# Hybrid decoder block on one core: two of four weight sums by accumulating DMAs, memory keys turned by TensorE

## The chip, the cores and the metric

The kernel runs on one core of a Trainium2 chip. Its time is the device time of one execution in microseconds (us). Engines are named TensorE (PE in the rows; PEld is its weight load), VectorE (DVE), ScalarE (ACT), GpSimd (POOL) and SyncE (SP, which here only issues DMAs; SPq is its queue). Each engine works through its own list of instructions in order and waits at semaphores for the others.

## The reference, cut to what matters

All is float32, with 256 tokens (S), 256 memory tokens and a model width of 2048.

```python
h = rmsnorm(x, g_mix[l])
z = h @ w_in[l]                       # 2048 x 12288: q|k|v, u|v, memory q, three gates
...
kvm = rmsnorm(mem, g_mem[l]) @ w_mem_kv[l]
km, vm = jnp.split(kvm, 2, axis=-1)
km = rmsnorm(km.reshape(B, M, N_HEADS_M, HEAD_DIM_M), gk_m[l])     # 4 heads of 256
...
merged = (ga * (ya @ w_branch[l, 0]) + gb * (yb @ w_branch[l, 1])
          + gm * (ym @ w_branch[l, 2]))
x = x + merged @ w_out[l]
hf = rmsnorm(x, g_ffn[l])
gt, up = jnp.split(hf @ w_gate_up[l], 2, axis=-1)                  # two halves of 5632 columns
x = x + (jax.nn.silu(gt) * up) @ w_down[l]
```

## The kernel before, in words

**Products.** A weight matrix comes in units of 512 KB (128 partitions x 2 blocks of 128 rows x 512 columns), one DMA each, issued by SP into one of six buffers `raw`. Each operand is split in two parts of type fp32r: ScalarE copies `raw` to `whi` (line 128), VectorE makes `wlo = raw - whi` (line 129), and each product is three matmuls, hi x hi, hi x lo, lo x hi. There are four `whi` and four `wlo` buffers. `product` (line 142) runs one column block of 512 for both halves of the tokens, 12 matmuls for a unit.

**The hidden stage.** `hidden(j)`, j from 0 to 10, makes 512 columns of the gate and the same 512 of the up projection with `fast_pair`. It walks over eight pairs of units, `src0[kp]` and `src1[kp]`. An ordinary pair costs 24 matmuls. For some pairs (`sums`) the 2x2 blocks of tokens and of weights are multiplied by a scheme of seven products in place of eight (21 matmuls), which needs four sums of weight blocks: `ta[0] = raw1[0] - raw0[0]`, `ta[1] = raw1[1] - raw1[0]`, `tb[0] = raw1[1] - ta[0]`, `tb[1] = raw0[1] - tb[0]`. `ta` and `tb` are then split like weights, into tiles `both`. The products are banks P1 to P7: P1 and P2 use raw0, P3 raw1, P5 and P7 use ta, P6 and P4 use tb. TensorE takes them in the order P1, P2, P3, P5, P7, P6, P4. Such sum blocks are the pairs 0, 2 and 4 for j from 2, pair 4 for j = 0, and pairs 0 and 4 for j = 1: 30 in all. After the last, `u2` to `u4` combine P1 to P7 on VectorE. `ta` lies in the pool's only buffer with tag "v"; the tile `v`, in which an activation is put together after its transposing DMA (`turn_end`, line 263), uses the same buffer. `tb` takes one of the six `raw` buffers.

**Around it.** `back` multiplies finished activations with w_down, between the hidden stages; its results are added into `xr` (line 634). Work handed to `defer` is emitted some units later.

**Turning.** To exchange rows and columns of a 128-row tile, `turn_start` splits it into two planes of 16-bit halves (VectorE, line 259) and SP issues transposing DMAs (line 261); `turn_end` joins the halves on ScalarE (line 265). `heads` does so with the normalised queries and keys, and VectorE then scales them by the gain (line 362).

**What sets the order.** The program is written in the order in which the functions are called; the tile framework's scheduler then sets each engine's list of instructions from it, by its own estimates of when what is ready, and places the semaphores. The instructions of a pair may therefore stand in another order than in the code.

Of the kernel before, what the change touches and what calls it, by code (L numbers as in the profile page):

```python
# [9 lines left out]
F32 = mybir.dt.float32  # L10
F32R = mybir.dt.float32r
U16 = mybir.dt.uint16
AF = mybir.ActivationFunctionType
ALU = mybir.AluOpType
AX = mybir.AxisListType

P = 128
S = 256
NT = S // P
# [10 lines left out]
NK = 2  # L30
# [8 lines left out]
def hybrid_block(ctx: ExitStack, tc: tile.TileContext, x, xT, memr, memT_in, gains, g_sgu, w_sguT, w_in, w_mem_kv,  # L39
                 w_branch, w_out, w_gate_up, w_down, out):  # L40
    nc = tc.nc

    cp = ctx.enter_context(tc.tile_pool(name="cp", bufs=1))
# [10 lines left out]
    def bigt(shape, dtype=F32, nm="big"):  # L54
        return big.tile(shape, dtype, tag="big", name=nm)
# [10 lines left out]
    def acct():  # L66
        return ps_acc.tile([P, NC], F32, tag="acc", name="acc")

    def smt():
        return ps_sm.tile([P, NC], F32, tag="sm", name="sm")  # L70
# [4 lines left out]

    gT = cp.tile([P, NGAIN], F32, name="gT")
    nc.scalar.dma_start(gT, gains)
    mhalf = cp.tile([P, 16], F32, name="mhalf")
    nc.vector.memset(mhalf, -0.5)
    warm = cp.tile([P, 16], F32, name="warm")  # L80
# [2 lines left out]
    for nm, n, s in (("qa", 1, 128.0 ** -0.5), ("qm", 2, 256.0 ** -0.5), ("b", 8, 0.5)):  # L83
# [9 lines left out]
                            pattern=[[-1, P]], channel_multiplier=1)  # L93
    nc.gpsimd.affine_select(out=dist[:, P:3 * P], in_=dist[:, P:3 * P], compare_op=ALU.is_ge, fill=1e33, base=P,
                            pattern=[[-1, 2 * P]], channel_multiplier=1)

    def gcol(nm, i=0):
        return gT[:, GAINS[nm] + i:GAINS[nm] + i + 1]
# [7 lines left out]
    def defer(f, units=1):  # L106

        later.append((clock[0] + units, f))
# [18 lines left out]
    def split_w(raw, hi, lo):  # L127
        nc.scalar.activation(hi, raw, AF.Copy)  # L128
        nc.vector.tensor_tensor(out=lo, in0=raw, in1=hi.bitcast(F32), op=ALU.subtract)  # L129
# [7 lines left out]
    def load_w(src):  # L137

        raw, hi, lo = unit_tiles()
        nc.sync.dma_start(raw, src.rearrange("p (k n) -> p k n", k=NK))  # L140
        split_w(raw, hi, lo)
        return hi, lo
# [28 lines left out]
    def fast_pair(src0, src1, quads, sums):  # L171

        P1, P2, P3, P5, P7, P6, P4, X = range(8)
        banks = {i: (ps_x.tile([P, NC], F32, tag="x", name="x") if i < 2 else acct()) for i in range(8)}  # L180
        npair = 2 * len(quads)
        uses = {b: [] for b in banks}
        for kp in range(npair):
            for b in (range(7) if kp in sums else (P2, P2, P3, P3, P4, P4, X, X)):
                uses[b].append(kp)
        done = {b: 0 for b in banks}

        def mm(b, a, w):

            first, done[b] = done[b] == 0, done[b] + 1  # L190
            last = done[b] == len(uses[b])
            nc.tensor.matmul(banks[b], a[0], w[0], start=first, stop=False)  # L192
            nc.tensor.matmul(banks[b], a[0], w[1], start=False, stop=False)  # L193
            nc.tensor.matmul(banks[b], a[1], w[0], start=False, stop=last)  # L194

        def split_t(t):
            both = bigt([P, 2, NK, NC], F32R, "both")
            split_w(t, both[:, 0], both[:, 1])
            return both[:, 0], both[:, 1]

        for kp in range(npair):
            q, c = quads[kp // 2], 2 * (kp % 2)

            def blk(i, t):
                return q[:, 0, c + i, t * P:(t + 1) * P], q[:, 1, c + i, t * P:(t + 1) * P]

            if kp not in sums:
                for src, b0, b1 in ((src0, P2, P4), (src1, P3, X)):
                    hi, lo = load_w(src[kp])
                    tick()  # L210
                    for i in range(NK):
                        w = hi[:, i, :], lo[:, i, :]
                        mm(b0, blk(i, 0), w)
                        mm(b1, blk(i, 1), w)
                continue
            sm = sums[kp]
            sk = [(sm[:, 0, i, :], sm[:, 1, i, :]) for i in range(4)]
            raw0, hi0, lo0 = unit_tiles()
            raw1, hi1, lo1 = unit_tiles()
            nc.sync.dma_start(raw0, src0[kp].rearrange("p (k n) -> p k n", k=NK))  # L220
            nc.sync.dma_start(raw1, src1[kp].rearrange("p (k n) -> p k n", k=NK))
            split_w(raw0, hi0, lo0)
            split_w(raw1[:, 1, :], hi1[:, 1, :], lo1[:, 1, :])
            ta = tr.tile([P, NK, NC], F32, tag="v", name="ta", bufs=1)
            tb = rawt().rearrange("p (k n) -> p k n", k=NK)
            nc.vector.tensor_tensor(out=ta[:, 0, :], in0=raw1[:, 0, :], in1=raw0[:, 0, :], op=ALU.subtract)
            nc.vector.tensor_tensor(out=ta[:, 1, :], in0=raw1[:, 1, :], in1=raw1[:, 0, :], op=ALU.subtract)  # L227
            nc.vector.tensor_tensor(out=tb[:, 0, :], in0=raw1[:, 1, :], in1=ta[:, 0, :], op=ALU.subtract)
            nc.vector.tensor_tensor(out=tb[:, 1, :], in0=raw0[:, 1, :], in1=tb[:, 0, :], op=ALU.subtract)
            tah, tal = split_t(ta)  # L230
            tbh, tbl = split_t(tb)
            tick()
            mm(P1, blk(0, 0), (hi0[:, 0, :], lo0[:, 0, :]))
            mm(P2, blk(1, 0), (hi0[:, 1, :], lo0[:, 1, :]))
            mm(P3, sk[3], (hi1[:, 1, :], lo1[:, 1, :]))
            mm(P5, sk[0], (tah[:, 0, :], tal[:, 0, :]))
            tick()
            mm(P7, sk[2], (tah[:, 1, :], tal[:, 1, :]))
            mm(P6, sk[1], (tbh[:, 0, :], tbl[:, 0, :]))
            mm(P4, blk(1, 1), (tbh[:, 1, :], tbl[:, 1, :]))  # L240
            if kp == max(sums):
                p1, p5, p6, p7 = (banks[b] for b in (P1, P5, P6, P7))
                c1, u2, u3, u4 = (wkt(nm) for nm in ("c1", "u2", "u3", "u4"))
                nc.scalar.activation(c1, p1, AF.Copy)
                for i, f in enumerate((lambda: add(u2, c1, p6), lambda: add(u4, u2, p5), lambda: add(u3, u2, p7),
                                       lambda: add(u2, u3, p5))):
                    defer(f, 0)
        for c, b in ((c1, P2), (u4, P3), (u3, P4), (u2, X)):
            add(c, c, banks[b])
        return c1, u4, u3, u2  # L250
# [81 lines left out]
    def head_norm(acc, rstd, hd):  # L332

        nh = NC // hd
        y = wkt("y")
        nc.scalar.activation(y, acc, AF.Identity, scale=rstd)
        sq = wkt("sq")
        nc.scalar.activation(sq, acc, AF.Square, scale=rstd)
        ss = stt(nh, "ss")
        nc.vector.tensor_reduce(out=ss, in_=sq.rearrange("p (h d) -> p h d", h=nh), axis=AX.X, op=ALU.add)  # L340
        nc.vector.tensor_scalar(ss, ss, 1.0 / hd, EPS, op0=ALU.mult, op1=ALU.add)
        r = stt(nh, "r")
        rpow(r, ss)
        y3 = y.rearrange("p (h d) -> p h d", h=nh)
        nc.vector.tensor_tensor(out=y3, in0=y3, in1=r[:, :, None].to_broadcast([P, nh, hd]), op=ALU.mult)
        return y

    def heads(dst, accs, rs, n, hd, g):

        turned = tr.tile([P, 2, 4, S], U16, tag="tr", name="turned")  # L350
        ys = [head_norm(accs[t], rs[t], hd) for t in range(NT)]

        def begin():
            for t in range(NT):
                turn_start(turned[:, :, :, t * P:(t + 1) * P], ys[t])

        def end():
            d = dst[:, 4 * n:4 * (n + 1), :]
            turn_end(d, turned)
            nj = hd // P  # L360
            for j in range(nj):
                nc.vector.tensor_scalar_mul(d[:, j:4:nj, :], d[:, j:4:nj, :], gcol(g, j))

        defer(begin)
        defer(end, 4)
# [23 lines left out]
    kmT = bigt([P, 2 * HM, S], F32, "kmT")  # L389
    vm = bigt([P, NT, WA], F32, "vm")  # L390
    hT = [quad("hT") for _ in range(4)]
    accs = product(w_mem_kv[0], memT, first=first)
    rstd_m = rows_rstd(memr, "m")
    defer(lambda: heads(kmT, accs, rstd_m, 0, 256, "km"))
    accs1 = product(w_mem_kv[1], memT)
    heads(kmT, accs1, rstd_m, 1, 256, "km")
    for i in range(4):
        defer(lambda i=i: quad_in(xT, i, hT[i], "mix"))
    rstd = rows_rstd(x, "x")
# [8 lines left out]
    for n in range(2):  # L408
        accs = product(w_in[COL_QM // NC + n], hT)
# [58 lines left out]
    for dst, col, g in ((qT, COL_Q, "qa"), (kT, COL_K, "ka")):  # L468
        for n in range(2):
            accs = product(w_in[col // NC + n], hT)  # L470
            heads(dst, accs, rstd, n, P, g)
    for n in range(2):
        accs = product(w_in[COL_V // NC + n], hT)
# [23 lines left out]
    def values(h):  # L497
# [13 lines left out]
                            pattern=[[0, 8], [1, P]], channel_multiplier=-1)  # L511
# [18 lines left out]
    for n in range(2):  # L530
        accs = product(w_in[COL_VB // NC + n], hT)
# [27 lines left out]
    for n in range(2):  # L559
        accs = product(w_in[COL_U // NC + n], hT)  # L560
# [8 lines left out]
    for n in range(D // NC):  # L569
        gates = []  # L570
        for b in range(3):
            accs = product(w_in[(COL_G + b * D) // NC + n], hT)
            gs = []
            for t in range(NT):
                g = wkt("gate")
# [5 lines left out]
        for i, (b, yq) in enumerate(((0, yA), (2, yM), (1, yB))):  # L581
            accs = product(w_branch[b, n], yq)
# [15 lines left out]
    for n in range(D // NC):  # L598
        accs = product(w_out[n], mT)
# [96 lines left out]
```

## Time and profile before

| | |
|---|---|
| median of 3 runs | 1589.76 us (1589.6 to 1593.58) |
| the profiled execution: its time, its span | 1587.5 us, 1585.7 us |
| TensorE busy | 1564.6 us, 99% |
| VectorE busy | 1099.8 us, 69% |
| ScalarE busy | 849.6 us, 54% |
| GpSimd busy | 31.4 us, 2% |
| granted TensorE clock | 0.999 |
| moved by DMA | 330.55 MB |

The span runs from the first to the last instruction. Matmuls are pipelined and each row's length overlaps the next one's, so the distance between the starts of two matmuls tells more than the length of one. An idle time in square brackets names the instruction that ended it.

### The profile page before, as it was taken

What the parts mean: (1) busy time and instruction counts of PE and PEld (TensorE: products, weight loads), DVE (VectorE), ACT (ScalarE), POOL (GpSimd) and SP (SyncE); (2) the same over time, 40 slices, a digit from 0 to 9 for tenths busy, and PEclk for the clock granted to TensorE, in tenths of its full rate; (3) what the DMA queues carried; (4) which work ended last, traced back from release to release, by engine and by line L of the source; (5) the groups of instructions that cost most, each with busy time, mean ns of one, the idle gap of its engine ahead of it and who ended that gap; (6) DMA issues with size and microseconds to landing.
All of it is one profiled execution on the core that took longest, in us unless ns stands there. A gap on an engine that the chain in (4) does not pass through costs nothing.

```text
span 1585.7 us, 18758 instructions
## 1 busy us (share of the span) xinstructions
PE 1564.6 (99%) x6886; PEld 1286.8 (81%) x6886; DVE 1099.8 (69%) x1329; ACT 849.6 (54%) x939; POOL 31.4 (2%) x33
## 2 busy tenths in 40 slices
PE   8999999999999999999999999999999999999998
PEld 6878887888888888888888887887878888888787
DVE  7756666677546464464676888787687786887965
ACT  6655756566545445444366555555455464555542
POOL 1001010000000000000000000000000000000000
PEclk9999999999999999999999999999999999999999
DMA  9787667665766667677676666576665665756763
GB/s 344 239 279 201 197 183 238 200 178 190 206 194 205 197 182 217 191 234 221 178 228 206 208 209 213 185 230 183 198 235 166 222 216 179 241 172 214 227 207 124
DMA packets 160749, 330.55 MB, mean 208 GB/s; under 512 B 83856, under 2 KB 84496, under 8 KB 160400
## 3 DMA queue, kind: packets, MB, share of 16 engines
q1 hardware_dynamic: 160512, 329.31, 66.5%
q8 instruction: 54, 0.88, 0.2%
q14 instruction: 39, 0.32, 0.1%
q10 hardware_dynamic: 144, 0.03, 0.0%
HBM read 309.36 MB, written 2.10 MB: 196 GB/s over the span
## 4 chain that ended last, share of the span: by engine, by line
PE 75%; DVE 12%; DMA 4%; issue 4%; ACT 3%; SPq 2%; POOL 1%; DVEq 0%; ACTq 0%; POOLq 0%
PE acc L154 17%; PE acc L155 17%; PE acc L153 16%; PE acc L193 6%; PE acc L194 6%; PE acc L192 6%; DVE wlo L129 5%; PE x L193 2%; PE x L194 2%; PE x L192 2%; DMA raw<-in_w_gate_up_dram 2%; SPq L261 1%; ACT whi L128 1%; DMA turned<-planes 1%; DVE xr L634 1%
## 5 line engine op out<-in xcount | busy, mean ns | idle before, releaser
L129 DVE TENSOR_TENSOR wlo<-raw,whi 128x1024 fp32r<-128x1024 f32 (+1 forms) x569 | 668.0, 1192 | 386.5 <-ACT whi L128 329.0
L128 ACT ACTIVATE whi<-raw 128x1024 fp32r<-128x1024 f32 (+1 forms) x569 | 574.6, 1030 | 449.1 <-PE acc L155 321.5
L153 PE MATMUL acc<-whi,hT 128*128 128x512 f32 x768 | 303.2, 395 | 0.0
L154 PE MATMUL acc<-wlo,hT 128*128 128x512 f32 x768 | 299.3, 390 | 1.4 <-DVE wlo L129 1.4
L155 PE MATMUL acc<-whi,hT 128*128 128x512 f32 x768 | 299.0, 389 | 0.0
L154 PEld LDWEIGHTS acc<-wlo,hT 128*128 128x128 f32 x768 | 144.3, 188 | 32.3 <-DVE wlo L129 2.9
L155 PEld LDWEIGHTS acc<-whi,hT 128*128 128x128 f32 x768 | 144.2, 188 | 30.1
L153 PEld LDWEIGHTS acc<-whi,hT 128*128 128x128 f32 x768 | 144.3, 188 | 29.6 <-ACT whi L128 0.3
L153 PE MATMUL acc<-whi,actT 128*128 128x512 f32 x352 | 136.9, 389 | 0.0
L155 PE MATMUL acc<-whi,actT 128*128 128x512 f32 x352 | 136.9, 389 | 0.0
L154 PE MATMUL acc<-wlo,actT 128*128 128x512 f32 x352 | 136.9, 389 | 0.0
L193 PE MATMUL acc<-wlo,x2T 128*128 128x512 f32 x348 | 135.5, 389 | 0.0
L192 PE MATMUL acc<-whi,x2T 128*128 128x512 f32 x348 | 135.5, 389 | 0.0
L194 PE MATMUL acc<-whi,x2T 128*128 128x512 f32 x348 | 135.4, 389 | 0.0
L128 ACT ACTIVATE both<-ta 128x1024 fp32r<-128x1024 f32 x30 | 31.9, 1064 | 101.4 <-DVE ta L227 101.4
L265 ACT ACTIVATE v<-turned 128x2048 uint16<-128x2048 uint16 x21 | 53.0, 2525 | 60.1 <-DMA turned<-planes 60.1
L154 PEld LDWEIGHTS acc<-wlo,actT 128*128 128x128 f32 x352 | 66.1, 188 | 13.9
L155 PEld LDWEIGHTS acc<-whi,actT 128*128 128x128 f32 x352 | 66.1, 188 | 13.7
L153 PEld LDWEIGHTS acc<-whi,actT 128*128 128x128 f32 x352 | 66.1, 188 | 13.6
L192 PEld LDWEIGHTS acc<-whi,x2T 128*128 128x128 f32 x348 | 65.3, 188 | 13.7
L193 PEld LDWEIGHTS acc<-wlo,x2T 128*128 128x128 f32 x348 | 65.3, 188 | 13.7
L194 PEld LDWEIGHTS acc<-whi,x2T 128*128 128x128 f32 x348 | 65.3, 188 | 13.6
(182 smaller groups left out, 2145.5 us busy)
## 6 DMA issues: line engine op xcount, KB each, us to landing
raw<-in_w_in_dram SPq DMA_DIRECT2D x192, 512.0 KB, 4.2
raw<-in_w_gate_up_dram SPq DMA_DIRECT2D x176, 512.0 KB, 3.8
raw<-in_w_down_dram SPq DMA_DIRECT2D x88, 512.0 KB, 4.2
raw<-in_w_branch_dram SPq DMA_DIRECT2D x48, 512.0 KB, 4.1
raw<-in_w_out_dram SPq DMA_DIRECT2D x32, 512.0 KB, 4.2
raw<-in_w_mem_kv_dram SPq DMA_DIRECT2D x31, 512.0 KB, 5.5
raw<-in_mem_dram SPq DMA_DIRECT2D x4, 512.0 KB, 6.1
raw<-in_xT_dram SPq DMA_DIRECT2D x4, 512.0 KB, 6.1
```

What stands on the lines that cost most here:

```text
L128: nc.scalar.activation(hi, raw, AF.Copy)
L129: nc.vector.tensor_tensor(out=lo, in0=raw, in1=hi.bitcast(F32), op=ALU.subtract)
L153: nc.tensor.matmul(accs[t], a_hi, hi[:, i, :], start=(k == 0), stop=False)
L154: nc.tensor.matmul(accs[t], a_hi, lo[:, i, :], start=False, stop=False)
L155: nc.tensor.matmul(accs[t], a_lo, hi[:, i, :], start=False, stop=(k == nk - 1))
L192: nc.tensor.matmul(banks[b], a[0], w[0], start=first, stop=False)
L193: nc.tensor.matmul(banks[b], a[0], w[1], start=False, stop=False)
L194: nc.tensor.matmul(banks[b], a[1], w[0], start=False, stop=last)
L261: nc.sync.dma_start_transpose(dst[:, h], planes[:, h, :])
L265: nc.scalar.activation(dst.bitcast(U16).rearrange("p c (s h) -> p h c s", h=2), planes, AF.Copy)
L634: nc.vector.tensor_tensor(out=xc[:, h], in0=xc[:, h], in1=accs[t][:, h], op=ALU.add)
```

## The change

Two edits are made. In `fast_pair`, `ta` is no longer made by two subtractions on VectorE: ScalarE writes the negated blocks `-raw0[0]` and `-raw1[0]` into `ta`, and GpSimd issues a DMA that reads the whole unit `src1[kp]` (512 KB) from HBM again and adds it onto `ta`. There are 30 such DMAs. In the memory keys' path, `heads_pe` takes the place of `heads`: TensorE turns each normalised tile by four transposes against an identity into a PSUM tile, and ScalarE moves it out, scaled by the gain.

```diff
+    ident = cp.tile([P, P], F32, name="ident")
+    nc.gpsimd.memset(ident, 0.0)
+    nc.gpsimd.affine_select(out=ident, in_=ident, compare_op=ALU.not_equal, fill=1.0, base=0,
+                            pattern=[[-1, P]], channel_multiplier=1)
...
-            nc.vector.tensor_tensor(out=ta[:, 0, :], in0=raw1[:, 0, :], in1=raw0[:, 0, :], op=ALU.subtract)
-            nc.vector.tensor_tensor(out=ta[:, 1, :], in0=raw1[:, 1, :], in1=raw1[:, 0, :], op=ALU.subtract)
+            nc.scalar.activation(ta[:, 0, :], raw0[:, 0, :], AF.Copy, scale=-1.0)
+            nc.scalar.activation(ta[:, 1, :], raw1[:, 0, :], AF.Copy, scale=-1.0)
+            nc.gpsimd.dma_start(ta, src1[kp].rearrange("p (k n) -> p k n", k=NK), accum_op=ALU.add)
             nc.vector.tensor_tensor(out=tb[:, 0, :], in0=raw1[:, 1, :], in1=ta[:, 0, :], op=ALU.subtract)
...
+    def heads_pe(dst, accs, rs, n, hd, g):
+
+        def turn_one(y, t):
+            ps = smt().rearrange("p (c s) -> p c s", c=4)
+            for c in range(4):
+                nc.tensor.transpose(ps[:, c, :], y[:, c * P:(c + 1) * P], ident)
+            nj = hd // P
+            for j in range(nj):
+                nc.scalar.activation(dst[:, 4 * n + j:4 * n + 4:nj, t * P:(t + 1) * P], ps[:, j:4:nj, :],
+                                     AF.Identity, scale=gcol(g, j))
+        for t in range(NT):
+            y = head_norm(accs[t], rs[t], hd)
+            defer(lambda y=y, t=t: turn_one(y, t), 2)
...
-    defer(lambda: heads(kmT, accs, rstd_m, 0, 256, "km"))
+    defer(lambda: heads_pe(kmT, accs, rstd_m, 0, 256, "km"))
     accs1 = product(w_mem_kv[1], memT)
-    heads(kmT, accs1, rstd_m, 1, 256, "km")
+    heads_pe(kmT, accs1, rstd_m, 1, 256, "km")
```

The order moves in the hidden stage as well. ScalarE's rows from the ordinary pair 1 over the sum block of pair 2 in hidden(2) were these (`whi` of the ordinary pair first, then of raw0 and of half of raw1, then the splits of ta and tb; in brackets the semaphores):

```order
L128 ACTIVATE whi_8103<-raw_8102 128x1024 [waits DMAHW5_49,PE_49,Activation_49]
L128 ACTIVATE whi_8121<-raw_8120 128x1024 [waits DMAHW6_49,PE_49,Activation_49]
L128 ACTIVATE whi_8139<-raw_8138 128x1024 [waits DMAHW7_49,PE_49,Activation_49]
L128 ACTIVATE whi_8142<-raw_8141 128x512 [waits DMAHW0_49,PE_49,Activation_49]
L128 ACTIVATE both_8156<-ta_8150 128x1024 [waits DVE_49]
L128 ACTIVATE both_8159<-raw_8151 128x1024 [waits DVE_49,PE_49]
L128 ACTIVATE whi_8184<-raw_8183 128x1024 [waits DMAHW1_49,PE_49,Activation_49]
```

ScalarE's rows at the same place now (the changed file's lines are 4 to 5 higher, and the buffers have other numbers):

```order
L132 ACTIVATE whi_8119<-raw_8118 128x1024 [waits DMAHW5_49,PE_49]
L132 ACTIVATE whi_8137<-raw_8136 128x1024 [waits DMAHW6_49,PE_49]
L132 ACTIVATE whi_8155<-raw_8154 128x1024 [waits DMAHW7_49,PE_49,Activation_49]
L230 ACTIVATE ta_8166<-raw_8154 128x512 [waits DVE_49]
L132 ACTIVATE whi_8158<-raw_8157 128x512 [waits DMAHW0_49,PE_49]
L231 ACTIVATE ta_8166<-raw_8157 128x512
L132 ACTIVATE both_8173<-ta_8166 128x1024 [waits DMASW7_49,Activation_49]
L132 ACTIVATE both_8176<-raw_8167 128x1024 [waits DVE_49,PE_49]
L132 ACTIVATE whi_8201<-raw_8200 128x1024 [waits DMAHW1_49,PE_49]
```

The two negated copies have come in, and the split of `ta` right behind them waits for the DMA (DMASW) in place of VectorE.

VectorE's rows behind the last sum block (pair 4) of hidden(2) were these (the second splits of ta and tb, then `wlo` of the ordinary pairs 5 and 6):

```order
L129 TENSOR_TENSOR both_8237<-ta_8231,both_8237 128x1024 [waits Activation_49]
L129 TENSOR_TENSOR both_8240<-raw_8232,both_8240 128x1024 [waits Activation_49]
L129 TENSOR_TENSOR wlo_8271<-raw_8269,whi_8270 128x1024 [waits DMAHW5_49,Activation_49]
L129 TENSOR_TENSOR wlo_8290<-raw_8288,whi_8289 128x1024 [waits DMAHW6_49,PE_49,Activation_49]
L129 TENSOR_TENSOR wlo_8309<-raw_8307,whi_8308 128x1024 [waits DMAHW7_49,Activation_49]
L253 TENSOR_TENSOR u2_8265<-c1_8264,acc_8054 128x512 [waits PE_49]
```

VectorE's rows at the same place now, from the first step of tb:

```order
L233 TENSOR_TENSOR raw_8249<-raw_8239,ta_8248 128x512 [waits DMASW0_49]
L234 TENSOR_TENSOR raw_8249<-raw_8236,raw_8249 128x512 [waits DVE_49]
L133 TENSOR_TENSOR both_8255<-ta_8248,both_8255 128x1024 [waits Activation_49]
L133 TENSOR_TENSOR both_8258<-raw_8249,both_8258 128x1024 [waits PE_49,Activation_49]
L258 TENSOR_TENSOR u2_8283<-c1_8282,acc_8069 128x512 [waits PE_49]
L133 TENSOR_TENSOR wlo_8289<-raw_8287,whi_8288 128x1024 [waits DMAHW5_49,Activation_49]
```

`u2`, which waits for TensorE, has moved ahead of the first `wlo` of pair 5, and the first step of `tb` waits for the DMA. On TensorE the first matmuls of P5, P7 and P6 in pair 4 now stand together, ahead of the second of P5.

## Rows read from the trace of the kernel before

**Rows 1.** The page: busy us (share of span) xinstructions; its main DMA queue.
```profile
PE 1564.6 (99%) x6886; PEld 1286.8 (81%) x6886; DVE 1099.8 (69%) x1329; ACT 849.6 (54%) x939; POOL 31.4 (2%) x33
...
q1 hardware_dynamic: 160512, 329.31, 66.5%
```

**Rows 2.** Windows: span; busy us (and count) by engine; granted clock, DMA share, GB/s.
```profile
1085.00:1110.00 25.00, 23.62 (x101) 18.36 (x101) 23.80 (x29) 14.34 (x18) 0.00 (x0) 1.00 0.69 211
900.00:1540.00 640.00, 632.41 (x2768) 517.64 (x2767) 516.58 (x592) 343.05 (x351) 0.00 (x0) 1.00 0.65 206
```

**Rows 3.** Timeline of TensorE in hidden(4): start, length, operation [idle before, releaser].
```profile
1085.73 0.39 PE L192 MATMUL x<-whi,x2T 128*128 128x512 f32 x1
...
1087.72 0.50 PE L193 MATMUL acc<-wlo,sums 128*128 128x512 f32 x1 [0.24 <-DVE wlo L129]
...
1090.67 0.50 PE L193 MATMUL acc<-both,sums 128*128 128x512 f32 x1 [0.60 <-DVE both L129]
...
1093.00 0.50 PE L193 MATMUL x<-wlo,x2T 128*128 128x512 f32 x1 [0.54 <-DVE wlo L129]
...
1094.96 0.40 PE L192 MATMUL acc<-whi,x2T 128*128 128x512 f32 x1
...
1098.37 0.39 PE L192 MATMUL x<-whi,x2T 128*128 128x512 f32 x1
...
1103.13 0.39 PE L192 MATMUL x<-whi,x2T 128*128 128x512 f32 x1
```

**Rows 4.** Timeline of ScalarE in the same stretch.
```profile
1084.22 1.07 ACT L128 ACTIVATE both<-ta 128x1024 fp32r<-128x1024 f32 x1 [3.12 <-DVE ta L227]
...
1089.26 3.46 ACT L128 ACTIVATE whi<-raw 128x1024 fp32r<-128x1024 f32 x4
1097.06 1.06 ACT L128 ACTIVATE both<-ta 128x1024 fp32r<-128x1024 f32 x1 [4.34 <-DVE ta L227]
```

**Rows 5.** Timeline of VectorE in the same stretch.
```profile
1080.63 1.22 DVE L125 SCALAR_TENSOR_TENSOR actT<-v,actT 128x1024 fp32r<-128x1024 f32 x1
...
1082.90 0.68 DVE L226 TENSOR_TENSOR ta<-raw 128x512 f32<-128x512 f32 x1
1083.51 0.68 DVE L227 TENSOR_TENSOR ta<-raw 128x512 f32<-128x512 f32 x1
...
1098.27 1.22 DVE L129 TENSOR_TENSOR both<-ta,both 128x1024 fp32r<-128x1024 f32 x1
```

**Rows 6.** Groups by line and form: busy us, mean ns | idle before.
```profile
L226 DVE TENSOR_TENSOR ta<-raw 128x512 f32<-128x512 f32 x30 | 20.5, 683 | 2.4 <-DMA raw<-in_w_gate_up_dram 2.4
...
L128 ACT ACTIVATE whi<-raw 128x512 fp32r<-128x512 f32 x32 | 19.7, 616 | 2.5 <-DMA raw<-in_w_mem_kv_dram 1.9 <-DMA raw<-in_w_gate_up_dram 0.6
```

**Rows 7.** Landing of raw0 (line 220), of raw1 (221), and the issues of xr.
```profile
DMA to landing us min/median/max: 3.4/3.8/6.4
...
DMA to landing us min/median/max: 3.2/3.7/7.1
...
xr<-in_x_dram SPq DMA_DIRECT2D x2, 1024.0 KB, 7.2
```

**Rows 8.** Groups of GpSimd: busy us, mean ns.
```profile
L101 POOL TENSOR_TENSOR r<-ss,mhalf 128x2 f32<-128x2 f32 x8 | 9.0, 1126 | 75.1 <-DVE ss L341 75.1
```

**Rows 9.** Timeline of SP's queue while memory keys are turned.
```profile
43.17 5.22 SPq L261 DMA_TRANSPOSE turned<-planes  x4
...
58.49 2.50 SPq L261 DMA_TRANSPOSE turned<-planes  x2
```

**Rows 10.** TensorE's waits up to 110 us (total, times, longest); one timeline row.
```profile
PE acc L154 <- DVE wlo L129: 2.6, 3, 1.5
...
84.22 0.50 PE L153 MATMUL acc<-whi,memT 128*128 128x512 f32 x1 [0.33 <-ACT whi L128]
```

**Rows 11.** Chain that ended last, near 390 us: start, length.
```profile
389.98 0.89 PE sm L552 x8
```

## The prediction

> **What bounds the kernel now.** I read the page's busy table first: TensorE is busy 1564.6 us of 1585.7 while VectorE has 69% and ScalarE 54% [rows 1]. So work taken from VectorE is worth only what TensorE waits for VectorE, and that is read from the stretch with the changed lines. In the windows view, VectorE is busy 23.80 of the 25 us from 1085 to 1110, the sum blocks of hidden(4); over the whole hidden stage it has slack [rows 2]. The timeline of TensorE for the same stretch gives the pitch: 36 matmuls from 1094.96 to 1103.13, or 0.227 us each, without a gap. Its only waits there are 0.24, 0.60 and 0.54 us, all for VectorE, in and just behind the first sum block (call it A, pair 0; B is pair 2, C pair 4) [rows 3]. That is 1.4 us in this stage. ScalarE idles before the splits of ta (3.12 us in A, 4.34 in B), until VectorE's second subtraction into ta [rows 4, 5]. Blocks B and C come without any TensorE wait, but with little room: B's second split of ta ends at 1098.27+1.22 = 1099.49 [rows 5], and TensorE uses it at 1098.37+10 x 0.227 = 1100.64 [rows 3].
>
> **What the change removes and adds.** VectorE loses two 512-wide subtractions for each of 30 sum blocks, 0.68 us each [rows 6], 41 us in all. They hid under TensorE except for the 1.4 us above, so at most some 13 us (nine such stages) can come back. ScalarE gains two 512-wide copies per block, 0.55 us each when issued back to back (four copies, one of them half as wide, take 3.46 us in [rows 4]; a single half one has 616 ns in [rows 6]).
>
> The price is the new wait. ScalarE's next instruction behind the two negated copies is the split of ta, which needs the accumulating DMA; so ScalarE stands, and behind it queue the splits of the ordinary pair that follows. VectorE stands at tb, and behind tb queue ta's and tb's second splits, then that pair's wlo. TensorE is fed by both. Call L the time from the end of the second negated copy to the data.
>
> Block A. The tile v must be free: VectorE's last read of it ends at 1080.63+1.22 = 1081.85 [rows 5], two copies make 1082.95, data at 1082.95+L. Two tb steps at the 0.6 us pitch and ta's split (1.15 pitch) end at 1085.35+L; TensorE would be there at 1085.73+10 x 0.227 = 1088.0. Then tb's split (1.15), two additions to xr (1.2) and one wlo (1.15) end at 1088.85+L, and there TensorE must start the ordinary pair's second matmul; it did so at 1093.00 [rows 3]. A costs L-4.15.
>
> Block B. ScalarE ends tb's split at 1085.25+L, then three 1024-wide copies (0.97 each) and three 512-wide ones: 1089.85+L; data at 1089.85+2L; ta's split ends 2.4 later, 1092.25+2L. TensorE arrives 34 matmuls (24 ordinary, 10 of the block) behind 1088.62+L, at 1096.33+L, so waits L-4.08, and begins pair 3 eleven matmuls after the split, 1094.74+2L, against 1103.13 before.
>
> Block C repeats it: tb's ScalarE split ends 1092.15+2L, six copies 1096.75+2L, data 1096.75+3L, ta's second split 1099.15+3L; TensorE arrives at 1094.74+2L+36 x 0.227 = 1102.9+2L, waits L-3.75, and starts pair 5 nine matmuls later, 1101.19+3L. Here the order adds a term that doesn't depend on L: u2 now stands ahead of the first wlo of pair 5 (before, three wlo stood ahead of it). u2 needs P6, whose last matmul ends at 1100.9+3L; u2 0.6-0.7 and wlo 1.15 end at 1102.75+3L, where TensorE is due at 1101.42+3L: 1.33 us more. Pair 5 effectively starts at 1102.52+3L against 1103.13+45 x 0.227 = 1113.33.
>
> So one hidden stage loses 3L-10.8 once L is above some 4.1. Nine stages (j from 2) have three blocks; hidden(0) has C alone, hidden(1) A and C: about 3(L-4.1)+2.7. Sum: 30L-107 us. Behind C the back stage runs at TensorE's pace and nothing is won back.
>
> **What L is.** No row of before shows a DMA issued by GpSimd or one that accumulates. From below: the same 512 KB loaded by SP landed in 3.2 us at the shortest, 3.7 to 3.8 in the median, and 7.1 at the longest [rows 7]. From above: an accumulation moves 512 KB of weights and must fetch 512 KB of ta, so 1 MB; the 1 MB load of xr took 7.2 us, and the smallest GpSimd operation has 1.1 us [rows 7, 8]: 8.3. With GpSimd's start the lower end is 3.8+1.1 = 4.9. It is one transfer in bytes of HBM and two in bytes handled, in a stretch where the DMA engines already have a share of 0.69 [rows 2], so I take the middle, 6.6: 30 x 6.6-107 = 91 us. The ends give 40 and 142.
>
> By the Trainium skill (DMA: Bandwidth & Descriptors, section "Issuing engines are not separate DMA queues") transfers from all engines run on the same 16 DMA engines and interleave, so GpSimd's queue would buy no bandwidth; no run here shows that yet, and it points to the upper end.
>
> **Memory keys.** Eight transposing DMAs, two ScalarE joins, four VectorE copies and four scalings go. SP held weight loads behind them for 5.22 us once and 2.50 us twice [rows 9], and the queue was then late: TensorE waits three times for a wlo, 2.6 us in all, and once 0.33 [rows 10]. If all go, 3.0 us come back. TensorE gains 16 transposes; 16 products of the same 128x128 f32 shape (x32 in the trace) cost four groups like that of 0.89 us [rows 11], 3.6 us. Net +0.6, from -1.2 (half the matmul cost) to +3.6. The eight ScalarE scalings of 256 columns replace the two joins, and GpSimd makes the identity at the start, under the first loads.
>
> **Sum.** 1587.5 (the profiled execution, 1.8 above its span) + 91 + 0.6 = 1679. The runs' median is 2.3 us above that execution, well inside the range.
>
> **Rivals.** *Quick landing:* the accumulation takes 3.2 us, as the shortest SP load [rows 7]. A then wins 0.95 per stage, B and C don't wait, u2 still costs 1.33: 9 x 0.38+1.7+0.6 = +6, so 1593. For it: ScalarE's idle before ta (3 to 4 us) would cover such an L. Against: only an undisturbed load did that. The Trainium skill (same page, section on the anatomy of one DMA by the GpSimd path) fits 2.0 us plus bytes at 436 GB/s, an estimate of 3.2 us for 512 KB; by it the time is this rival's.
>
> *VectorE relief (the other side):* if data came within 2.65 us, A's waits go as well (1.4 x 9 = 12.5 us), the keys win 3, and were u2's wait hidden by a VectorE that is ahead, 1572; with it (1.33 in eleven stages) 1587. It decides at L = 2.65, below every 512 KB landing seen; the order of u2 speaks against it too.
>
> *Slow accumulation:* the read-modify-write goes at a fraction of a load's rate, L of 10 or more, from contention with the loads at share 0.69: 30 x 12-107 = +253, 1841 for L = 12. For it: 7.1 us landings occur already. Against: queue 1 has a third of its time free [rows 1], and loads, paced by freed buffers, would thin out while ScalarE and VectorE stand.
>
> **How the numbers follow.** Forecast case (L from 4.4 to 9.2) 0.78: 25 to 169 us, 1612 to 1757. Quick landing or L up to 4.4: 0.09, half of it within 0.3% (some 5 us, about what a measurement of this kernel can tell from no change). Relief 0.04, mostly faster. Slow accumulation 0.09. So faster 0.03, same 0.06, slower 0.91; the range 1612 to 1760 leaves the three rivals out, 2 in 10.
>
> **What would show it.** ScalarE's idle before both<-ta should be ended by the DMA of ta and be close to L in B and C; VectorE's before tb likewise; TensorE should wait at P5 in all three blocks, and once more at pair 5's first wlo. GpSimd's issues should land in 5 to 8 us. Stages before the first hidden one should be as long as now within 3 us. The forecast is wrong if ta lands under 4 us, or if the weight loads, not ScalarE, end the new waits.

## The result

| | before | after |
|---|---|---|
| median (range, runs) | 1589.89 us (1589.6 to 1593.58, 4) | 1725.1 us (1721.85 to 1728.65, 4) |
| ratio, 95% interval | | 1.0848 [1.0829, 1.0868] |
| profiled execution: time, span | 1587.5, 1585.7 us | 1723.5, 1721.8 us |
| granted TensorE clock | 0.999 | 0.972 |

The changed kernel is 135 us slower; 1679 was forecast, from 1612 to 1760.

The page of the changed kernel: busy us (share) xinstructions, two DMA queues, the shares of the chain that ended last, groups (busy us, mean ns | idle before, releaser), and the landing of the new DMA.

```profile
PE 1620.7 (94%) x6902; PEld 1314.8 (76%) x6902; DVE 1061.9 (62%) x1261; ACT 878.3 (51%) x1005; POOL 57.0 (3%) x65
...
q1 hardware_dynamic: 156160, 328.26, 60.9%
q0 software_dynamic: 4320, 15.73, 5.2%
...
PE 56%; DMA 17%; DVE 12%; issue 6%; ACT 6%; SPq 2%; POOL 0%; DVEq 0%; ACTq 0%; POOLq 0%
...
L233 DVE TENSOR_TENSOR raw<-raw,ta 128x512 f32<-128x512 f32 x30 | 20.8, 692 | 179.1 <-DMA ta<-in_w_gate_up_dram 179.1
L132 ACT ACTIVATE both<-ta 128x1024 fp32r<-128x1024 f32 x30 | 31.7, 1057 | 162.2 <-DMA ta<-in_w_gate_up_dram 162.2
...
ta<-in_w_gate_up_dram POOLq DMA_DIRECT2D x30, 512.0 KB, 7.6
```

Against [rows 1], VectorE is 38 us less busy, as the edit intends, and that helps nothing: each of 30 blocks makes VectorE idle 6.0 us and ScalarE 5.4 us until the DMA of `ta` has landed. The median landing is 7.6 us behind the issue. TensorE is busy 56 us *longer*, with hardly more instructions; most of that is the lower clock, to which I come below.

One hidden stage shows the chain. The timeline of ScalarE: its negated copies (lines 230, 231) and the splits of `ta`, in the three sum blocks A, B and C.

```profile
1202.15 0.62 ACT L231 ACTIVATE ta<-raw 128x512 f32<-128x512 f32 x1
1210.55 1.06 ACT L132 ACTIVATE both<-ta 128x1024 fp32r<-128x1024 f32 x1 [6.32 <-DMA ta<-in_w_gate_up_dram]
...
1216.78 0.61 ACT L231 ACTIVATE ta<-raw 128x512 f32<-128x512 f32 x1
1226.03 1.06 ACT L132 ACTIVATE both<-ta 128x1024 fp32r<-128x1024 f32 x1 [8.63 <-DMA ta<-in_w_gate_up_dram]
...
1232.32 0.62 ACT L231 ACTIVATE ta<-raw 128x512 f32<-128x512 f32 x1
1239.13 0.60 ACT L249 ACTIVATE c<-x 128x512 f32<-128x512 f32 x1 [6.20 <-PE x L198]
1240.76 1.06 ACT L132 ACTIVATE both<-ta 128x1024 fp32r<-128x1024 f32 x1 [1.02 <-DMA ta<-in_w_gate_up_dram]
```

From the end of the second negated copy to VectorE's first use of the data (0.06 us before the split shown) L is 7.72, 8.58 and 7.76 us here; over all 30 blocks it averages 7.98, from 5.8 to 9.5. In C the idle time is divided, since the copy of P1 (line 249) stands in between. TensorE in the same stage:

```profile
1211.66 0.50 PE L196 MATMUL acc<-both,sums 128*128 128x512 f32 x1 [2.49 <-ACT both L132]
1213.10 0.79 PE L197 MATMUL acc<-both,sums 128*128 128x512 f32 x1 [0.94 <-DVE both L133]
1213.69 0.63 PE L198 MATMUL acc<-both,sums 128*128 128x512 f32 x1
1214.12 0.63 PE L196 MATMUL acc<-both,sums 128*128 128x512 f32 x1
...
1219.10 0.40 PE L196 MATMUL acc<-whi,x2T 128*128 128x512 f32 x1
1219.33 0.39 PE L197 MATMUL acc<-wlo,x2T 128*128 128x512 f32 x1
...
1227.14 0.49 PE L196 MATMUL acc<-both,sums 128*128 128x512 f32 x1 [1.07 <-ACT both L132]
1228.57 0.50 PE L197 MATMUL acc<-both,sums 128*128 128x512 f32 x1 [0.94 <-DVE both L133]
...
1241.87 0.73 PE L196 MATMUL acc<-both,sums 128*128 128x512 f32 x2 [1.41 <-ACT both L132]
...
1247.30 0.50 PE L197 MATMUL x<-wlo,x2T 128*128 128x512 f32 x1 [0.56 <-DVE wlo L133]
```

It waits at P5 in A, B and C, where [rows 3] has waits in A alone, and once more at pair 5's first `wlo`. After A's waits the pitch is 0.43 us, not 0.227, up to 1218.81. The windows of the changed kernel say why: columns as in [rows 2].

```profile
1205.00:1210.00 5.00, 4.17 (x19) 3.12 (x17) 0.58 (x1) 0.00 (x0) 0.00 (x0) 1.00 0.77 176
1210.00:1215.00 5.00, 2.40 (x6) 1.70 (x7) 4.47 (x6) 4.12 (x5) 0.00 (x0) 0.71 0.32 105
1215.00:1220.00 5.00, 5.00 (x15) 3.93 (x14) 4.46 (x5) 2.40 (x4) 0.87 (x1) 0.61 0.75 230
1220.00:1225.00 5.00, 5.00 (x23) 4.13 (x22) 0.00 (x0) 0.00 (x0) 0.00 (x0) 1.00 0.90 190
```

The granted clock falls from 1.00 to 0.71 and 0.61 around the waits and is back at 1.00: for some 6 us TensorE ran at the lower level, 1.2 GHz in place of 2.4. Over the kernel, TensorE's waits from the first hidden stage on sum to 90.3 us:

```profile
PE acc L196 <- ACT both L132: 62.7, 37, 4.1
PE acc L197 <- DVE both L133: 16.6, 19, 0.9
PE x L197 <- DVE wlo L133: 5.8, 9, 1.0
PE x L196 <- DVE c L258: 5.2, 2, 2.8
```

Before, the same waits are some 7 us. So in TensorE's own account 83 us more are waits and 56 us longer busy time, 139 where the span grew by 136. Of the 56 some 40 are slow matmuls: 221 of them start 0.30 to 0.46 us behind the one before in place of 0.227. The rest is length that no next matmul covers, beside the waits.

### The profile page after: what moved, and what is told of

Its sections match the earlier page's. It is cut to its first block, busy times and chain, and to the rows that moved or that the text cites. A ratio compares the mean times of both kernels' runs of the same rounds, so it can differ in the third digit from the quotient of the medians.

```text
span 1721.8 us, 18870 instructions
## 1 busy us (share of the span) xinstructions
PE 1620.7 (94%) x6902; PEld 1314.8 (76%) x6902; DVE 1061.9 (62%) x1261; ACT 878.3 (51%) x1005; POOL 57.0 (3%) x65
## 4 chain that ended last, share of the span: by engine, by line
PE 56%; DMA 17%; DVE 12%; issue 6%; ACT 6%; SPq 2%; POOL 0%; DVEq 0%; ACTq 0%; POOLq 0%
PE acc L158 15%; PE acc L159 15%; PE acc L157 15%; DMA ta<-in_w_gate_up_dram 13%; DVE wlo L133 5%; ACT whi L132 3%; PE acc L198 2%; PE acc L197 2%; PE acc L196 2%; SPq L266 2%; DMA turned<-planes 1%; DVE raw L233 1%; DVE raw L234 1%; DMA raw<-in_w_gate_up_dram 1%; PE x L197 1%
## 5 line engine op out<-in xcount | busy, mean ns | idle before, releaser
L233 DVE TENSOR_TENSOR raw<-raw,ta 128x512 f32<-128x512 f32 x30 | 20.8, 692 | 179.1 <-DMA ta<-in_w_gate_up_dram 179.1
L196 PE MATMUL acc<-both,sums 128*128 128x512 f32 x90 | 46.5, 533 | 62.7 <-ACT both L132 62.7
L196 PEld LDWEIGHTS acc<-both,sums 128*128 128x128 f32 x90 | 20.7, 237 | 82.0 <-ACT both L132 78.4
L197 PE MATMUL x<-wlo,x2T 128*128 128x512 f32 x176 | 71.5, 406 | 5.9 <-DVE wlo L133 5.8
L196 PEld LDWEIGHTS acc<-whi,x2T 128*128 128x128 f32 x348 | 66.0, 190 | 14.1 <-ACT whi L132 0.2
L159 PEld LDWEIGHTS acc<-whi,actT 128*128 128x128 f32 x352 | 66.1, 188 | 13.8
```

Of the source, the lines that this page charges most:

```text
L159: nc.tensor.matmul(accs[t], a_lo, hi[:, i, :], start=False, stop=(k == nk - 1))
```

## Experiments

To compare stages, the table takes the start of the copy of P1 (`c1`), which every hidden stage has once, in the third and in the eleventh stage, and divides the difference by eight. Each ratio is to the kernel before on the same chip, where its median was 1589.74 to 1593.84 us.

| kernel | third, eleventh | a stage, us | median, us | ratio to before, interval |
|---|---|---|---|---|
| before | 980.60, 1495.83 | 64.40 | | |
| after | 1001.56, 1628.85 | 78.41 | 1725.1 | 1.0848 [1.0829, 1.0868] |
| keys_only | 981.61, 1494.97 | 64.17 | 1587.9 | 0.9972 [0.9961, 0.9983] |
| sums_only | 1004.25, 1634.25 | 78.75 | 1732.72 | 1.0882 [1.0854, 1.0911] |
| unawaited | 983.21, 1497.44 | 64.28 | 1589.68 | 0.9984 [0.9971, 0.9997] |
| plain_dma | 996.13, 1582.66 | 73.32 | 1672.2 | 1.0503 [1.0477, 1.0529] |
| half | 997.97, 1557.09 | 69.89 | 1645.38 | 1.0339 [1.0319, 1.0359] |
| b_only | 981.02, 1552.06 | 71.38 | 1641.39 | 1.0311 [1.029, 1.0333] |
| early | 1004.36, 1610.40 | 75.76 | 1699.99 | 1.0687 [1.067, 1.0704] |
| early2 | 997.93, 1566.22 | 71.04 | 1656.04 | 1.0388 [1.0368, 1.0409] |
| early3 | 998.12, 1530.11 | 66.50 | 1621.9 | 1.0181 [1.0159, 1.0203] |
| early4 | 994.98, 1511.82 | 64.61 | 1601.82 | 1.0076 [1.0063, 1.009] |

**keys_only and sums_only** undo one edit each. keys_only makes `ta` by the two subtractions again:

```diff
-            nc.scalar.activation(ta[:, 0, :], raw0[:, 0, :], AF.Copy, scale=-1.0)
-            nc.scalar.activation(ta[:, 1, :], raw1[:, 0, :], AF.Copy, scale=-1.0)
-            nc.gpsimd.dma_start(ta, src1[kp].rearrange("p (k n) -> p k n", k=NK), accum_op=ALU.add)
+            nc.vector.tensor_tensor(out=ta[:, 0, :], in0=raw1[:, 0, :], in1=raw0[:, 0, :], op=ALU.subtract)
+            nc.vector.tensor_tensor(out=ta[:, 1, :], in0=raw1[:, 1, :], in1=raw1[:, 0, :], op=ALU.subtract)
```

> Only the memory keys are turned by TensorE; ta is made by VectorE as before. My theory: the keys' edit is worth 1.5 us, since hidden(0) began at 869.15 in the changed kernel against 870.67 before, so 1588 +- 2. Rival: part of the 135 us comes from the keys' edit (SP's loads reordered, other buffers), then above 1600.

sums_only turns the memory keys by `heads` again:

```diff
-    defer(lambda: heads_pe(kmT, accs, rstd_m, 0, 256, "km"))
+    defer(lambda: heads(kmT, accs, rstd_m, 0, 256, "km"))
...
-    heads_pe(kmT, accs1, rstd_m, 1, 256, "km")
+    heads(kmT, accs1, rstd_m, 1, 256, "km")
```

> Only ta is made by the negated copies and the accumulating DMA; the keys are turned as before. My theory: the whole loss is here, 1726 +- 4, with a period of 78 us per hidden stage (65 before). Rival: the two edits act together, then below 1700.

The loss lies wholly in the sums (+139.8 us against before on the same chip; the 1732.72 us are 2.7 above the range expected). The keys' edit wins a little, 0.28%, and keys_only, the fastest version here, beats both kernels. The two edits don't visibly act on each other: 1.0882 x 0.9972 = 1.085, the ratio of the changed kernel. That keys_only takes the 1588 us expected is no proof of the 1.5 us, as before has 1592.92 on that chip, and the reason given for them did not hold: the first hidden matmul of keys_only starts at 870.86 us, as late as before (870.67), and the 869.15 of the changed kernel lies within the spread of the kernels with this edit (868.8 to 873.2).

**unawaited** keeps VectorE's sums and adds the same 30 accumulating DMAs, onto a tile that nobody reads; nothing of the reference is left out.

```diff
-    tr = ctx.enter_context(tc.tile_pool(name="tr", bufs=2))
+    tr = ctx.enter_context(tc.tile_pool(name="tr", bufs=1))
...
+            nc.vector.tensor_tensor(out=ta[:, 0, :], in0=raw1[:, 0, :], in1=raw0[:, 0, :], op=ALU.subtract)
+            nc.vector.tensor_tensor(out=ta[:, 1, :], in0=raw1[:, 1, :], in1=raw1[:, 0, :], op=ALU.subtract)
+            nc.gpsimd.tensor_copy(dm[:, 0, 0:1], ta[:, 0, 0:1])
+            nc.gpsimd.dma_start(dm, src1[kp].rearrange("p (k n) -> p k n", k=NK), accum_op=ALU.add)
```

> The keys' edit alone (ta by VectorE), and beside it the same 30 accumulating DMAs of 512 KB, each issued when its ta is ready, onto a tile that nobody reads (the output is that of the reference; the transposing buffers are one in place of two, to make room). My theory: the wait costs, not the traffic, so 1588 to 1595. Rival: the 15.7 MB more in the DMA engines delay the weight loads, then 1650 or more.

Its windows over the hidden stages (columns as in [rows 2]):

```profile
900.00:1540.00 640.00, 631.36 (x2761) 516.05 (x2760) 516.25 (x591) 342.76 (x351) 49.85 (x58) 1.00 0.77 230
```

Its page, on the landing of the weight loads there and of the added DMAs:

```profile
raw<-in_w_gate_up_dram SPq DMA_DIRECT2D x176, 512.0 KB, 4.5
...
dm<-in_w_gate_up_dram POOLq DMA_DIRECT2D x30, 512.0 KB, 7.2
```

The DMA share rises from 0.65 [rows 2] to 0.77 and the landing takes nearly as long as in the changed kernel (7.2 us against 7.6), but a stage keeps its 64.3 us (64.2 in keys_only). So the transfers themselves cost at most the 1.8 us between the medians of unawaited and keys_only; the wait for them costs the rest. The loads next to them land in 4.5 us in place of 3.8, so the transfers do meet, but the loads have that time in hand. The Trainium skill has transfers of all issuing engines run on the same 16 DMA engines and interleave (DMA: Bandwidth & Descriptors, section "Issuing engines are not separate DMA queues"); this trace agrees.

**plain_dma** lets the DMA overwrite `ta` instead of adding, so it leaves the subtraction out of `ta`.

```diff
-            nc.gpsimd.dma_start(ta, src1[kp].rearrange("p (k n) -> p k n", k=NK), accum_op=ALU.add)
+            nc.gpsimd.dma_start(ta, src1[kp].rearrange("p (k n) -> p k n", k=NK))
```

> The changed kernel with the same DMA without the addition: it overwrites ta with the unit (so ta lacks the subtraction). If the reading and adding of ta makes the DMA slow, the landing falls from 7.6 to some 4.9 us and by 30L-107 the time to some 1630. If it is GpSimd's way of issuing and the loads beside it, the landing stays at 7 to 8 us and the time at 1700 to 1725.

**half** makes only `ta[0]` by a DMA, of 256 KB.

```diff
-            nc.scalar.activation(ta[:, 1, :], raw1[:, 0, :], AF.Copy, scale=-1.0)
-            nc.gpsimd.dma_start(ta, src1[kp].rearrange("p (k n) -> p k n", k=NK), accum_op=ALU.add)
+            nc.gpsimd.dma_start(ta[:, 0, :], src1[kp][:, 0:NC], accum_op=ALU.add)
+            nc.vector.tensor_tensor(out=ta[:, 1, :], in0=raw1[:, 1, :], in1=raw1[:, 0, :], op=ALU.subtract)
```

> Only the first of the two sums of each block is made by an accumulating DMA (256 KB instead of 512 KB); the second is VectorE's subtraction as before, and ScalarE's second negated copy is gone. Theory A (the landing is mostly bytes at the rate of the accumulating write): landing falls from 7.6 us to about 4.5 to 5.5 and the kernel to 1610 to 1660 us. Theory B (the landing is mostly a fixed time from issue to data): landing stays at 6.5 us or more, and with one copy of 0.6 us less ahead of it the kernel takes 1670 to 1715 us.

Both tell what L is made of. First plain_dma, then half: the landing, from the view of the issuing line, and the queue of GpSimd's DMAs, from the page (packets, MB, share of 16 engines):

```profile
DMA to landing us min/median/max: 3.9/5.3/8.5
...
q0 software_dynamic: 4320, 15.73, 2.5%
```

```profile
DMA to landing us min/median/max: 3.9/6.4/8.7
...
q0 software_dynamic: 4320, 7.87, 2.7%
```

Without the addition the median landing falls from 7.6 to 5.3 us and the average L to 6.1; the 1672 us lie between the two times that were expected. With half the bytes the landing falls only to 6.4, L to 6.9: the time is theory A's, the landing nearly B's.

The shares of queue q0 split the landing. Share x span / 30 is the time for which each of the 16 DMA engines handles packets of one such DMA: 3.0 us in the changed kernel (5.2%), 1.4 without the addition, 1.5 with half the bytes. So the addition doubles the packets' time, and that time goes with the bytes. What is left of the landing, 4.6, 3.9 and 4.9 us, does not go with the bytes; the number of packets is the same in all three, so whether it goes with that is open. These are estimates: the same DMA of 512 KB landed in a median of 7.1 us in early2 and 8.5 in b_only, with other work beside it.

How L enters a stage can be read block by block. In eight of the nine full stages of the changed kernel, the time from A's data to B's and from B's to C's is L+6.9 us, within 0.1; so it is in plain_dma. There L is 6.22 in place of 8.07 in the mean of the eight stages, and 3 x 1.85 = 5.6 us were to be won of a stage; it is 5.1 us shorter. half won more, 8.5 us, than its L of 6.95 gives (3 x 1.1 = 3.4): from data to data it takes L+5.0, since ScalarE no longer has the second negated copy and has one `whi` copy and a half behind the issue in place of ahead of it (twice 1.9 us), and from C's data to the next A's copy another 1.3 us less. That makes 8.5.

**b_only** uses the DMA for pair 2 alone.

```diff
+            if kp == 2:
                 nc.scalar.activation(ta[:, 0, :], raw0[:, 0, :], AF.Copy, scale=-1.0)
                 ...
+            else:
+                nc.vector.tensor_tensor(out=ta[:, 0, :], in0=raw1[:, 0, :], in1=raw0[:, 0, :], op=ALU.subtract)
+                nc.vector.tensor_tensor(out=ta[:, 1, :], in0=raw1[:, 1, :], in1=raw1[:, 0, :], op=ALU.subtract)
```

> The accumulating DMA for pair 2 of each stage alone (the middle one of its three sum blocks); the other blocks are subtracted by VectorE as before; the edit to the keys stays. Theory (the wait of a block less the slack that stood before it, each block for itself): 7.9 less about 4.1 is 3.6 us a stage, so 32 us in nine or ten stages and 1620 us, with TensorE's weight-ready waits only in the middle block. Rival 1 (a block alone is forgiven by the slack of its neighbours, and only a chain of three costs): under 1600 us. Rival 2 (most of the loss is a lower clock after any wait): over 1640 us.

TensorE in one such block:

```profile
1177.96 0.39 PE L198 MATMUL acc<-whi,sums 128*128 128x512 f32 x1
1181.49 0.79 PE L196 MATMUL acc<-both,sums 128*128 128x512 f32 x1 [3.14 <-ACT both L132]
1182.93 0.79 PE L197 MATMUL acc<-both,sums 128*128 128x512 f32 x1 [0.65 <-DVE both L133]
...
1187.65 0.39 PE L196 MATMUL x<-whi,x2T 128*128 128x512 f32 x1
```

The granted clock there (columns as in [rows 2]):

```profile
1180.00:1185.00 5.00, 2.87 (x6) 1.98 (x7) 4.60 (x5) 4.23 (x5) 0.00 (x0) 0.57 0.37 105
1185.00:1190.00 5.00, 5.00 (x18) 3.96 (x18) 4.97 (x8) 1.85 (x3) 0.00 (x0) 0.75 0.91 293
```

A lone block costs 71.38-64.40 = 7.0 us a stage, not 3.6. Its waits are 3.14+0.65 = 3.8. That is near the 3.6 by luck: the DMA landed later here, in 8.5 us in the median, and with this block's L of 8.8 the slack formula gives 4.7. But from 1181.49 to 1187.65 twelve matmuls take 6.16 us; less the 0.65, and 12 x 0.227 = 2.72 at full clock, that leaves 2.8 us for the lower clock. So rival 2 was half right, and the 1641 us are just past its bound: where no further wait comes, the slow matmuls are paid for in full.

**early** issues loads, negated copies and DMA of a block one pair earlier. **early2** adds a second buffer for `ta` and `v` and holds VectorE's `tb` and ScalarE's split of `ta` behind the block's ordinary splits. **early3** issues them ahead of the block before (seven `raw` buffers). **early4** also starts a stage's first block ahead of the last product of `back`.

In early:

```diff
         for kp in range(npair):
+            if kp + 1 in sums:
+                staged[kp + 1] = stage(kp + 1)
...
+            raw0, raw1, ta = staged.pop(kp) if kp in staged else stage(kp)
```

> Loads, negated copies and the accumulating DMA of each sum block are issued one weight pair earlier; the arithmetic and the number of DMAs are unchanged. Theory (the stage loses the time in which ScalarE and VectorE wait for the block ta, so an earlier start gives it back as far as buffers allow): the loss of a hidden stage falls from 12.8 us to about 6 or 7, since ScalarE's four ordinary copies now lie under the landing, but the single buffer of ta still chains the blocks: 1655 to 1680 us, and ScalarE's wait for ta before both<-ta falls from 162 us in 30 to under 90. Rival (the transfers or the lower clock cost the time wherever they stand): within 10 us of 1725.

In early2, besides the buffers:

```diff
-            split_w(raw1[:, 1, :], hi1[:, 1, :], lo1[:, 1, :])
+            a, v = split_w(raw1[:, 1, :], hi1[:, 1, :], lo1[:, 1, :])
...
+            with tc.issue_after(a.ins), tc.issue_after(v.ins):
+                nc.vector.tensor_tensor(out=tb[:, 0, :], in0=raw1[:, 1, :], in1=ta[:, 0, :], op=ALU.subtract)
```

> As the run with the accumulating DMA issued one pair earlier, but ta and v have two buffers (turned one in place of two), and VectorE's first step of tb and ScalarE's split of ta are held behind the ordinary pair's copies and remainders, so that nothing ordinary queues behind the wait. Theory (only the wait at the head of an in-order queue costs time; the landing itself is free when other work lies under it): blocks B and C lose about 1 to 2 us each, since the negated copies still stand behind the block before, A about 3, so 5 to 7 us a stage in place of 14 and 1635 to 1665 us. Rival (the time is lost to the transfer or to VectorE's and ScalarE's total work): above 1690 as before.

In early3, ahead of these instructions:

```diff
+            if kp + 2 in sums:
+                staged[kp + 2] = stage(kp + 2)
```

> As the run before it, and the loads, negated copies and DMA of the next sum block are issued before the splits of the present one, with a seventh raw buffer (taken from the pool of the large tiles, 13 in place of 14). Theory: B and C no longer wait at all, only A (whose unit cannot come earlier) loses some 3 us a stage: 1600 to 1630 us. Were A covered too, VectorE's relief would show and the time fall below 1590. Rival 1 (raw buffers held longer make the loads late): TensorE's waits are then for wlo or whi released by the loads of raw, and the time is above 1650. Rival 2 as before, above 1690.

In early4, in `back`:

```diff
+            if nxt and n == ns[-1]:
+                begun = stage_block(w_gate_up[nxt][0], w_gate_up[NFF + nxt][0])
```

> As the run before it, and the first block of a stage (pair 0, from the third stage on) is begun one w_down column block ahead, behind the activation's tile v and before the last product of the back stage. Theory: the landing of all three blocks lies under other work, no wait for ta is left from the third stage on, and a stage takes 64.4 us or, with VectorE's two subtractions gone, down to 63: 1585 to 1605 us (the first two stages still lose some 8). Rival (with the DMA hidden, the splits of ta and tb that ScalarE and VectorE hand each other still end TensorE's waits in A): 66 us a stage and 1610 to 1620.

early won only 25 us, less than expected, and ScalarE's wait for `ta`, expected under 90 us, is still 155.9; the other three came out within their ranges. The timeline of VectorE in early shows why:

```profile
1207.02 1.22 DVE L133 TENSOR_TENSOR wlo<-raw,whi 128x1024 fp32r<-128x1024 f32 x1
1214.30 0.69 DVE L246 TENSOR_TENSOR raw<-raw,ta 128x512 f32<-128x512 f32 x1 [6.06 <-DMA ta<-in_w_gate_up_dram]
1214.91 2.96 DVE L133 TENSOR_TENSOR wlo<-raw,whi 128x1024 fp32r<-128x1024 f32 x3
```

The scheduler had put the first step of `tb` ahead of three ordinary `wlo`, so VectorE waited with ready work behind it, and TensorE for that `wlo` (3.29 us at 1216.18). ScalarE, whose four copies did come first, idled 5.12 us before B's split. With the order mended and two buffers (early2), stages take 71.0 us; with the chain from block to block cut as well (early3) 66.5; with the first block begun early (early4) 64.6, with the landing still at a median of 7.7 us. TensorE's waits in early4 from 995 to 1600 us:

```profile
PE x L207 <- DVE wlo L133: 4.1, 8, 0.5
PE acc L207 <- DVE both L133: 1.4, 3, 0.7
```

VectorE's second split of `tb` in A of one of these stages, and TensorE's two waits there:

```profile
1105.04 1.23 DVE L133 TENSOR_TENSOR both<-raw,both 128x1024 fp32r<-128x1024 f32 x1 [1.13 <-ACT both L132]
...
1106.32 0.50 PE L207 MATMUL acc<-both,sums 128*128 128x512 f32 x1 [0.72 <-DVE both L133]
1108.65 0.50 PE L207 MATMUL x<-wlo,x2T 128*128 128x512 f32 x1 [0.54 <-DVE wlo L133]
```

The totals are what the kernel before has (4.3 and 1.3 us from 1000 to 1560 us), though VectorE was relieved of two subtractions in each block. VectorE idles 1.13 us before the second split of `tb` until ScalarE has made the first, and TensorE then waits 0.72+0.54 us: the waits of A in this stage come from the hand-over between the two engines, and fewer VectorE instructions did not shorten it. So with the price gone the edit's possible gain did not appear in this order of instructions; another order of the steps of `tb` was not tried. The 12 us that early4 is still over before lie between the `c1` of the first and that of the third stage: the two intervals take 50.8 and 49.2 us where before has 40.6 and 43.9. There a sum block meets the additions of the stage's end, for which TensorE waits on VectorE (5.9 us, in two); the rest of it was not taken apart.

## Why the forecast was near, and where it was off

**The chain was right.** The signs named ahead are there: ScalarE and VectorE are released by the DMA of `ta` in nearly all blocks, TensorE waits in A, B and C and at pair 5, GpSimd's DMAs land in 5.5 to 9.2 us, a little over the 5 to 8 named. For the stage shown, 3L-10.8 gives 7.72+8.58+7.76-10.8 = 13.3 us, and the stage takes 77.95, 13.6 over the 64.40 of before. The steps inside hold too: from A's data to B's L+6.9 = 15.48 was reckoned and 15.48 measured, from B's to C's 14.66 against 14.73, and L+6.9 holds in eight of nine stages. And unawaited, plain_dma, b_only and the four early kernels show by intervention that it is the wait, at the head of in-order queues and chained from block to block, that is paid.

**The term that was mis-sized is L**: 6.6 taken, 7.98 measured (bounds 4.9 to 8.3). In the step "What L is" the middle was chosen between rows of other DMAs. With 7.98 the sum is 30 x 7.98-107 = 132 us in place of 91. plain_dma and half show what was missing: the addition costs 2.3 us of landing, 1.6 of it in the time of the packets, and some 4 to 5 us of a landing do not go with the bytes, so that neither SP's loads (3.8 us [rows 7]) nor the bytes could give it. The upper bound, which counted twice the bytes, was the nearer one. Both bounds also took 1.1 us as the smallest GpSimd operation, which it is not (the kernel before has some of 0.1 to 0.6 us); the changed kernel has 0.3 us from the copy's end to the issue and 0.87 for issuing, so that this part came out near is luck. The landings measured, 5.3 us plain and 7.6 accumulating, among other transfers, refute the rival of quick landing. The Trainium skill's fit (DMA: Bandwidth & Descriptors, section "Anatomy of one DMA — SWDGE (gpsimd) path"), 2.0 us plus bytes at 436 GB/s, gives an estimate of 3.2 us for 512 KB; the measurement differs, and decides.

**What was not forecast:** twice, the longer time in hidden(1), TensorE waits, 5.2 us in all, for the additions to `c`, queued on VectorE behind its own wait for `ta`. 132+5.2, less 1.5 by which the first hidden matmul comes earlier (869.15 against 870.67), makes 136, the measured difference of the two profiled executions. The agreement is partly luck: u2's term was 1.33 us by reckoning and 0.56 in the row above, so other small terms make up some 0.8 a stage, and the 1.5 us are no effect of the keys' edit but lie in the spread between kernels, as keys_only shows.

**TensorE's own waits were forecast too long**, 4.5 us in B where 1.07+0.94 were seen. It arrives late, having run 13 matmuls at a pitch 0.2 us longer after A: 2.0+2.6 = 4.6. That the slow clock did not lengthen the stage is argued from this and from the chain's intervals, which hold without it; b_only shows that it does cost 2.8 us where nothing else sets the pace. The forecast has no term for the clock at all, and that the chain hid it was luck.

**Keys.** +0.6 was taken, and keys_only gained. The 16 transposes take 2.4 us, not 3.6 (four in 0.60 us, where I had taken 0.89 for four [rows 11]), and TensorE's waits for `wlo` up to 110 us [rows 10] are gone: the first matmul with `hT` comes at 97.36 instead of 99.69. At the first hidden matmul nothing of that is left (870.86 against 870.67), and the spans of the profiled executions differ by 1.1 us; how the rest of the 5.0 us between the medians (interval 2.7 to 6.2) comes about stays open, since before ranged from 1587.17 to 1597.09 on that chip.

**VectorE relief** fell twice: the shortest landing in the changed kernel was 5.5 us, far from 2.65, and early4, where the landing is hidden, wins nothing from it.

## To carry to other kernels

Handing a sum to a DMA is priced by its landing, of which the packets' time was here the smaller part (3.0 of 7.6 us): count the time from the last instruction ahead of the issue to the data, and ask which in-order queue has its head at that wait and what ready work stands behind. If the landing can't be put under other work (an earlier start, a second buffer, and the waiter placed behind the ordinary work), leave the sum on the engine; and before any of that, check that the relieved engine is what the bottleneck waits for, since a hand-over between two others looks the same in the list of waits.

## Unexpected of the hardware

An accumulating 512 KB DMA from GpSimd landed in 7.6 us in the median, a plain one in 5.3, a 256 KB accumulating one in 6.4; the packets' time on each DMA engine was 3.0, 1.4 and 1.5 us. GpSimd spent 0.87 us on issuing an accumulating one and 0.54 on a plain one. And behind waits of 2.5 and 0.9 us TensorE's granted clock fell, to 0.61 from 1215 to 1220 us, while in early4, whose waits from 1000 to 1560 us are at most 0.7 us, it is 1.00 over that stretch.
